# Turned outputs of a retention head ahead of three products, gated outputs in pairs, angle tables one stage earlier

## The chip, the cores and the metric

One core of one Trainium2 chip runs one layer of a decoder trunk. The metric is the time of one execution on the device in microseconds; of several runs the median counts. Profiles are of one execution.

## The reference, cut to what matters

The layer has two branches on the same normalised input (512 tokens, 1024 channels), then an output projection, an MLP and a gated input embedding. The change touches the retention branch, the start of the stage of the other branch's projection, and the start of the output projection:

```python
rq = rope(rq.reshape(B, S, RET_HEADS, RET_QK_DIM), pos)
rk = rope(rk.reshape(B, S, RET_HEADS, RET_QK_DIM), pos) * (RET_QK_DIM ** -0.5)
ro = retention(rq, rk, rv)          # 4 heads, key width 256, value width 512
ro = rms_norm(ro, ret_norm.reshape(RET_HEADS, RET_V_DIM)).reshape(B, S, RET_V_W)
a_ret = (ro * jax.nn.silu(rg)) @ w_br
...
a_mla = mo @ w_bm                   # mo: output of the 8-head latent attention
mixed = jax.nn.sigmoid(gr) * a_ret + jax.nn.sigmoid(gm) * a_mla
x = x + mixed @ w_o
```

`rope` turns the two halves of each head's query and key by cosines and sines of position times frequency; for the retention heads these are the angle tables of this document.

## The kernel before, in words

Every product is of float32 values split into two parts: ScalarE rounds a tile to its high part (lines 262, 307, 310), VectorE takes the remainder as its low part (266, 268, 308, 313), and TensorE does three matmuls (low by high, high by low, high by high) into one PSUM bank. Weights come as chunks of 512 KB through SyncE's and GpSimd's DMA queues into six raw buffers and are split into three pairs of buffers (`wh_...`, `wl_...`). A full product of one weight chunk is 24 matmuls.

The program is a list of steps in an order written out by hand. Each step names the weight chunk that it uses; when the list is run, the chunk of the next step is asked for ahead of the step. Matmuls, and some transfers and table functions, are held in program order (`keep_in_program_order`). The order of all else on each engine is made by a planner, which takes what is ready, the earlier in the program first. PSUM has eight banks under one tag (`psum`, line 162), most activations share 43 buffers of one tag (`dyn`).

The stages around the change, in order of time:

- Latent attention, head by head; the last gate products `gr`; then the projection `bm` of the attention output in eight steps (`branch_m`), with the input x loaded, scaled and split again between them (`norm_x`, tiles `xr`, `xn`). `ret_angles` loads the positions (`posr`) and reduces the angles (`trig`, tiles `tra`, `trk`), `ret_sincos` takes sine and cosine on ScalarE and makes the table `tab`. They stand after steps 2 and 4 of `bm`.
- Retention, two heads at a time (`for q in range(RH // 2)`). For all heads but the first, query and key come from a seven-product scheme: `qk(h, p)` is one product, p being 1, 7, 2, 6, 5, 4, 3 in some order, of 24 matmuls of 256 columns each; products 2, 5, 4 and 3 finish a block of query or key, which VectorE turns with the angle table (763, 847 to 855) and which is then split (`rqx`, `rqy`, `rkx`, `rky`). `seven("rv", ...)` and `seven("rg", ...)` are the same for values and gates, two weight chunks to each product.
- A head goes through `ret_scores`, `ret_attend` (four output blocks `o` and their sums of squares), `ret_gated` (four instructions on VectorE, line 891: output by norm by gate), `ret_turned` (16 transposes `ot` into four banks, each split into `rog` tiles with the norm's gain, lines 310 and 313) and `branch(h, 0..3)` (`branch_r`, products with `w_br`, added up over the heads in DRAM for all but the last).
- After the last head the parts are mixed (`mix`, tiles `mix0` to `mix7`), and the output projection `wo` begins with half a product of its first two chunks (`out_part`).

In the loop, `ret_turned(h)` of the first head of a pair stands right ahead of its branch, behind qk products 5, 4 and 3 of the next head. `ret_turned` of the second head of the first pair stands one product ahead of its branch, and its gated outputs ahead of all products of the next pair.

Of the kernel before, what the change touches and what calls it, by code (L numbers as in the profile page):

```python
# [40 lines left out]
RH, RQK, RV = 4, 256, 512  # L41
# [107 lines left out]
def trunk_layer(ctx: ExitStack, tc: tile.TileContext, xT, pT, pos, gains, const, decay, wstream, outT):  # L149
# [52 lines left out]
    offset, o = {}, 0  # L202
# [5 lines left out]
    def step(key, fn, *args):  # L208
        steps.append((key, fn, args))
# [675 lines left out]
            d["o"].append(o)  # L885
        d["r"], _ = mean_rsqrt(f"ro{h}", ss.rearrange("p (b c) -> p b c", c=1), RV)

    def ret_gated(h):
        d = R[h]
        for b in range(4):  # L890
            STT(d["o"][b], d["o"][b], d["r"][:, b:b + 1], d["z"][b], op0=ALU.mult, op1=ALU.mult)

    def ret_turned(h):
# [260 lines left out]
    def fill(n=1):  # L1154
        for _ in range(n):
            if fillers and fillers[0][0] is None:
                step(*fillers.pop(0))
            if fillers:
                step(*fillers.pop(0))
# [77 lines left out]
    step(None, attend, MH - 1)  # L1237
    step(None, mo_split, MH - 2)
    fill(len(fillers))
    step(None, norm_x, 0)  # L1240
    step(None, norm_x, 1)
    step(None, mo_split, MH - 1)
    for n in range(8):
        step(("bm", n), branch_m, n)
        if n < 6:
            step(None, norm_x, 2 + n)
        if n in (2, 4):
            step(None, ret_angles if n == 2 else ret_sincos)
        if n == 3:
            step(None, x_operand, 7)  # L1250
    for p in (1, 2, 4):
        step(None, x_operand, p)
    def qk(h, *ps):
        for p in ps:
            step(("sw", ("qk", h), p, 0), ret_qk7, h, p)

    def seven(kind, q, *ps):
        for p in ps:
            for c in range(2):
                step(("sw", (kind, q), p, c), ret_seven, kind, q, p, c)  # L1260

    def branch(h, *ks):
        for k in ks:
            step(("br", h, k), branch_r, h, k)


    for q in range(RH // 2):
        h = 2 * q
        if q:
            qk(h, 1, 7, 2, 6)  # L1270
            step(None, ret_turned, h - 1)
            qk(h, 5)
            branch(h - 1, 0)
            qk(h, 4, 3)
            branch(h - 1, 1)
            seven("rv", q, 1)
            branch(h - 1, 2)
            step(None, ret_scores, h)
            seven("rv", q, 7, 2, 6)
            branch(h - 1, 3)  # L1280
        else:
            for key in ("rq", "rk"):
                for n in range(2):
                    step((key, h, n), ret_qk, h, key, n)
            for p, x in ((1, 6), (7, 5), (2, 3)):
                seven("rv", q, p)
                step(None, x_operand, x)
            seven("rv", q, 6)
            step(None, ret_scores, h)
        seven("rv", q, 5, 4, 3)  # L1290
        seven("rg", q, 1)
        step(None, ret_attend, h)
        seven("rg", q, 7, 2, 6)
        qk(h + 1, 1, 7)
        seven("rg", q, 5)
        qk(h + 1, 2)
        seven("rg", q, 4)
        step(None, ret_gated, h)
        qk(h + 1, 6)
        seven("rg", q, 3)  # L1300
        qk(h + 1, 5, 4, 3)
        step(None, ret_turned, h)
        branch(h, 0, 1)
        step(None, ret_scores, h + 1)
        step(None, odd_v, h + 1)
        branch(h, 2, 3)
        step(None, ret_attend, h + 1)
        step(None, ret_gated, h + 1)
    for n in range(8):
        step(None, reload, n)  # L1310
    for n in range(EARLY, 8):
# [2 lines left out]
            step(None, ret_turned, RH - 1)  # L1314
    for k in range(4):
        step(("br", RH - 1, k), branch_r, RH - 1, k)
        step(None, mix, 2 * k)
        step(None, mix, 2 * k + 1)
    for n in range(2):
        step(("o", n), out_part, n, 0)  # L1320
    for n in range(8):
        step(("o", n), out_proj, n)
    step(None, open_tail)
# [106 lines left out]
```

## Time and profile before

| | |
|---|---|
| median of 3 runs | 1125.55 us (1125.17 to 1126.24) |
| profiled execution, its own time | 1122.77 us |
| its span, first to last instruction | 1121.0 us |
| TensorE busy | 1096.8 us (98%) |
| VectorE busy | 730.2 us (65%) |
| ScalarE busy | 558.1 us (50%) |
| mean granted clock of TensorE | 0.993 of full |

The share of an engine is its busy time over the span. The time of a run is a little longer than the span, since it holds what lies before the first and after the last instruction. The granted clock is what the throttle let through, 1.00 being full speed.

### The profile page before, as it was taken

What the parts mean: (1) busy time and instruction counts of PE and PEld (TensorE: products, weight loads), DVE (VectorE), ACT (ScalarE), POOL (GpSimd) and SP (SyncE); (2) the same over time, 40 slices, a digit from 0 to 9 for tenths busy, and PEclk for the clock granted to TensorE, in tenths of its full rate; (3) what the DMA queues carried; (4) which work ended last, traced back from release to release, by engine and by line L of the source; (5) the groups of instructions that cost most, each with busy time, mean ns of one, the idle gap of its engine ahead of it and who ended that gap; (6) DMA issues with size and microseconds to landing.
All of it is one profiled execution on the core that took longest, in us unless ns stands there. A gap on an engine that the chain in (4) does not pass through costs nothing. (4 is left out here: it accounts for less than half of the span.)

```text
span 1121.0 us, 14372 instructions
## 1 busy us (share of the span) xinstructions
PE 1096.8 (98%) x5353; PEld 920.0 (82%) x5353; DVE 730.2 (65%) x1178; ACT 558.1 (50%) x805; POOL 100.6 (9%) x133
## 2 busy tenths in 40 slices
PE   9999999999999989999998999999999999999998
PEld 7878888887788868888886887888888888888887
DVE  7697587557784763765477368555466566668685
ACT  7637555545455644554554634334443443445552
POOL 0000000001112102122110200010100100101000
PEclk9999999999999989999998999999999999999999
DMA  7242232366778865498894944693855755738511
GB/s 258 67 137 75 79 87 85 123 227 205 184 208 224 225 200 153 140 237 215 204 224 165 243 151 153 204 270 116 173 162 171 173 167 155 184 130 211 146 57 57
DMA packets 62166, 186.18 MB, mean 166 GB/s; under 512 B 7632, under 2 KB 9040, under 8 KB 61840
## 3 DMA queue, kind: packets, MB, share of 16 engines
q1 hardware_dynamic: 45744, 131.49, 34.5%
q0 software_dynamic: 16208, 53.75, 24.7%
q8 instruction: 42, 0.69, 0.2%
q14 instruction: 28, 0.23, 0.1%
q10 hardware_dynamic: 144, 0.03, 0.0%
HBM read 166.10 MB, written 17.04 MB: 163 GB/s over the span
## 5 line engine op out<-in xcount | busy, mean ns | idle before, releaser
L169 PE MATMUL dn<-wh_dn,cl 128*128 128x512 f32 x224 | 87.2, 389 | 0.0
L169 PE MATMUL dn<-wh_dn,ch 128*128 128x512 f32 x224 | 87.1, 389 | 0.0
L169 PE MATMUL dn<-wl_dn,ch 128*128 128x512 f32 x224 | 87.1, 389 | 0.0
L262 ACT ACTIVATE wh_dn<-wr_dn 128x1024 fp32r<-128x1024 f32 x32 | 34.0, 1062 | 75.4 <-PE up L169 54.3
L262 ACT ACTIVATE wh_up<-wr_up 128x1024 fp32r<-128x1024 f32 x32 | 34.0, 1061 | 57.7 <-PE up L169 29.3
L266 DVE TENSOR_TENSOR wl_dn<-wr_dn,wh_dn 128x1024 fp32r<-128x1024 f32 x32 | 39.0, 1220 | 27.5 <-ACT wh_dn L262 27.5
L266 DVE TENSOR_TENSOR wl_up<-wr_up,wh_up 128x1024 fp32r<-128x1024 f32 x32 | 39.1, 1222 | 18.6 <-ACT wh_up L262 18.6
L169 PEld LDWEIGHTS dn<-wh_dn,ch 128*128 128x128 f32 x224 | 42.0, 188 | 8.8
L1022 DVE SCALAR_TENSOR_TENSOR f<-up,bcx 128x512 f32<-128x512 f32 x32 | 20.6, 686 | 44.0 <-PE up L169 44.0
L169 PEld LDWEIGHTS dn<-wl_dn,ch 128*128 128x128 f32 x224 | 42.0, 188 | 8.7
L169 PEld LDWEIGHTS dn<-wh_dn,cl 128*128 128x128 f32 x224 | 42.0, 188 | 8.6
L224 POOL DMA_DIRECT2D dr_dn<-wstream x24 | 21.5, 894 | 289.6 <-DMA dr_dn<-wstream 165.7
L262 ACT ACTIVATE wh_dn<-dr_dn 128x1024 fp32r<-128x1024 f32 x24 | 25.5, 1061 | 42.1 <-PE up L169 29.0
L266 DVE TENSOR_TENSOR wl_dn<-dr_dn,wh_dn 128x1024 fp32r<-128x1024 f32 x24 | 29.4, 1223 | 22.4 <-ACT wh_dn L262 22.4
L262 ACT ACTIVATE wh_rv<-wr_rv 128x1024 fp32r<-128x1024 f32 x28 | 29.6, 1058 | 25.7 <-PE rv L169 10.6
L262 ACT ACTIVATE wh_rg<-wr_rg 128x1024 fp32r<-128x1024 f32 x28 | 29.6, 1058 | 25.6 <-PE rg L169 18.9
L266 DVE TENSOR_TENSOR wl_rg<-wr_rg,wh_rg 128x1024 fp32r<-128x1024 f32 x20 | 24.5, 1226 | 23.3 <-ACT wh_rg L262 23.3
L266 DVE TENSOR_TENSOR wl_rv<-wr_rv,wh_rv 128x1024 fp32r<-128x1024 f32 x20 | 24.4, 1223 | 16.0 <-ACT wh_rv L262 16.0
L1080 DVE TENSOR_TENSOR d<-d,dn 128x1024 f32<-128x1024 f32 x24 | 29.3, 1219 | 6.4 <-PE dn L169 6.4
L266 DVE TENSOR_TENSOR wl_br<-wr_br,wh_br 128x1024 fp32r<-128x1024 f32 x16 | 19.5, 1221 | 20.2 <-ACT wh_br L262 20.2
L262 ACT ACTIVATE wh_qk<-wr_qk 128x1024 fp32r<-128x1024 f32 x21 | 22.3, 1063 | 19.7 <-DMA wr_qk<-wstream 7.3
L911 ACT ACTIVATE rt<-br 128x512 f32<-128x512 f32 x24 | 14.0, 595 | 33.1 <-PE br L169 30.7
(1928 smaller groups left out, 3569.5 us busy)
## 6 DMA issues: line engine op xcount, KB each, us to landing
wr_up<-wstream SPq DMA_DIRECT2D x32, 512.0 KB, 4.3
wr_dn<-wstream SPq DMA_DIRECT2D x32, 512.0 KB, 3.5
dr_dn<-wstream POOLq DMA_DIRECT2D x24, 512.0 KB, 7.8
wr_rv<-wstream SPq DMA_DIRECT2D x20, 512.0 KB, 4.6
wr_rg<-wstream SPq DMA_DIRECT2D x20, 512.0 KB, 4.8
wr_rv<-wstream POOLq DMA_DIRECT2D x16, 512.0 KB, 7.6
wr_rg<-wstream POOLq DMA_DIRECT2D x16, 512.0 KB, 7.5
wr_br<-wstream SPq DMA_DIRECT2D x16, 512.0 KB, 5.1
```

What stands on the lines that cost most here:

```text
L169: return tc.keep_in_program_order(nc.tensor.matmul(*a, **k))
L224: nc.gpsimd.dma_start(raw, chunk(("w", blk, kb, fb, c)), accum_op=ALU.add)
L262: i = ACT(hi, raw, AF.Copy, scale=sign)
L266: TT(lo, raw, hi.bitcast(F32), op=ALU.subtract)
L911: ACT(t, ps, AF.Copy)
L1022: STT(u[:, i], ps[:, i], 0.0, V["bcx2"], op0=ALU.max, op1=ALU.mult)
L1080: TT(to, to, dps[p], op=ALU.add if sign > 0 else ALU.subtract)
```

## The change

Four things move; no instruction's shape changes. The angles of the retention tables are reduced ahead of the `bm` stage, and the sines and cosines are taken after its first step. At the start of the second pair the gated outputs of head 1 are made two at a time between the products, their transposes stand behind product 2, and a value product and product 6 lie between them and the branch; branch chunks 1 and 2 follow product 3. In each pair the first head's transposes move ahead of products 5, 4 and 3. In the output projection the first half product stands ahead of the last two mixes in the list.

```diff
-    def ret_gated(h):
+    def ret_gated(h, bs=(0, 1, 2, 3)):
         d = R[h]
-        for b in range(4):
+        for b in bs:
             STT(d["o"][b], d["o"][b], d["r"][:, b:b + 1], d["z"][b], op0=ALU.mult, op1=ALU.mult)
...
     fill(len(fillers))
+    step(None, ret_angles)
     step(None, norm_x, 0)
     step(None, norm_x, 1)
     step(None, mo_split, MH - 1)
...
         step(("bm", n), branch_m, n)
         if n < 6:
             step(None, norm_x, 2 + n)
-        if n in (2, 4):
-            step(None, ret_angles if n == 2 else ret_sincos)
+        if n == 0:
+            step(None, ret_sincos)
...
         if q:
-            qk(h, 1, 7, 2, 6)
+            qk(h, 1)
+            step(None, ret_gated, h - 1, (0, 1))
+            qk(h, 7)
+            step(None, ret_gated, h - 1, (2, 3))
+            qk(h, 2)
             step(None, ret_turned, h - 1)
-            qk(h, 5)
+            seven("rv", q, 1)
+            qk(h, 6)
             branch(h - 1, 0)
-            qk(h, 4, 3)
-            branch(h - 1, 1)
-            seven("rv", q, 1)
-            branch(h - 1, 2)
+            qk(h, 5, 4, 3)
+            branch(h - 1, 1, 2)
             step(None, ret_scores, h)
             seven("rv", q, 7, 2, 6)
             branch(h - 1, 3)
...
         seven("rg", q, 3)
+        step(None, ret_turned, h)
         qk(h + 1, 5, 4, 3)
-        step(None, ret_turned, h)
         branch(h, 0, 1)
         step(None, ret_scores, h + 1)
         step(None, odd_v, h + 1)
         branch(h, 2, 3)
         step(None, ret_attend, h + 1)
-        step(None, ret_gated, h + 1)
+    step(None, ret_gated, RH - 1)
...
     for k in range(4):
         step(("br", RH - 1, k), branch_r, RH - 1, k)
+        if k == 3:
+            step(("o", 0), out_part, 0, 0)
         step(None, mix, 2 * k)
         step(None, mix, 2 * k + 1)
-    for n in range(2):
-        step(("o", n), out_part, n, 0)
+    step(("o", 1), out_part, 1, 0)
```

## Rows read from the trace of the kernel before

**Rows 1.** The page's busy table, TensorE: busy us, share, instructions.
```profile
PE 1096.8 (98%) x5353; PEld 920.0 (82%) x5353; DVE 730.2 (65%) x1178; ACT 558.1 (50%) x805; POOL 100.6 (9%) x133
```
**Rows 2.** Waits of TensorE, whole span: us in total, times, longest.
```profile
PE br L169 <- ACT rog02h L310: 3.2, 1, 3.2
...
PE rq L169 <- ACT xn7h L307: 2.5, 1, 2.5
...
PE br L169 <- DVE rog11l L313: 0.8, 1, 0.8
```
**Rows 3.** Windows: stretch, busy us (instructions) by engine, PEclk, DMA share, GB/s.
```profile
414.00:420.00 6.00, 5.21 (x12) 3.74 (x13) 2.11 (x4) 1.05 (x2) 1.44 (x2) 0.50 0.74 166
420.00:426.00 6.00, 6.00 (x28) 4.97 (x27) 1.23 (x1) 2.14 (x3) 1.11 (x2) 1.00 0.33 115
280.00:285.00 5.00, 3.90 (x16) 3.02 (x17) 4.52 (x7) 3.38 (x6) 0.56 (x1) 1.00 0.85 217
397.38:416.12 18.74, 13.67 (x95) 11.62 (x94) 18.00 (x30) 9.68 (x14) 1.73 (x2) 0.92 0.59 168
...
240.00:245.00 5.00, 5.00 (x24) 4.13 (x22) 3.34 (x5) 1.75 (x3) 1.08 (x2) 1.00 0.69 256
```
**Rows 4.** Timeline of TensorE, head 0's turned outputs and branch: start, us, what.
```profile
405.56 1.91 PE L169 MATMUL ot<-cst,o 128*128 128x128 f32 x16
...
420.22 0.40 PE L169 MATMUL br<-rog02h,wl_br 128*128 128x512 f32 x1
...
425.90 0.39 PE L169 MATMUL br<-rog02l,wh_br 128*128 128x512 f32 x1
```
**Rows 5.** Timeline of TensorE, head 2's turned outputs and branch.
```profile
602.04 1.91 PE L169 MATMUL ot<-cst,o 128*128 128x128 f32 x16
...
614.67 0.40 PE L169 MATMUL br<-rog20h,wh_br 128*128 128x512 f32 x1
```
**Rows 6.** Timeline of TensorE, start of the second pair.
```profile
457.10 0.28 PE L169 MATMUL qk<-xn7h,wh_qk 128*128 128x256 f32 x1
458.77 0.39 PE L169 MATMUL qk<-s60h,wl_qk 128*128 128x256 f32 x1 [1.39 <-DVE wl_qk L266]
...
461.74 1.91 PE L169 MATMUL ot<-cst,o 128*128 128x128 f32 x16
463.41 0.36 PE L169 MATMUL qk<-s50h,wl_qk 128*128 128x256 f32 x1
```
**Rows 7.** Timeline of ScalarE, angle tables and head 0's branch.
```profile
275.18 1.28 ACT L492 ACT_TABLE_LOAD   x1
...
412.15 0.63 ACT L307 ACTIVATE rkx1h<-rku 128x512 fp32r<-128x512 f32 x1 [2.72 <-DVE rku L854]
```
**Rows 8.** Timeline of VectorE, angle table and head 1's gated outputs.
```profile
278.32 0.43 DVE L495 TENSOR_SCALAR tab<-tab 128x512 f32<-128x512 f32 x1 [1.48 <-ACT tab L494]
...
454.85 2.74 DVE L891 SCALAR_TENSOR_TENSOR o<-o,ro,z 128x512 f32<-128x512 f32 x4
```
**Rows 9.** Timeline of TensorE, first retention query product.
```profile
277.86 0.39 PE L169 MATMUL rq<-xn6h,wh_rq 128*128 128x512 f32 x1
...
281.94 0.40 PE L169 MATMUL rq<-xn7h,wh_rq 128*128 128x512 f32 x1
```
**Rows 10.** Timeline of SyncE, VectorE and TensorE, start of the projection stage.
```profile
228.06 0.42 SPq L718 DMA_DIRECT2D xr<-xT  x1
...
231.28 0.69 DVE L308 TENSOR_TENSOR mos7l<-mo,mos7h 128x512 fp32r<-128x512 f32 x1 [0.90 <-ACT mos7h L307]
...
234.80 0.39 PE L169 MATMUL bm<-mos7l,wh_bm 128*128 128x512 f32 x1
```
**Rows 11.** Window of the instructions on the angle tile alone: VectorE, ScalarE.
```profile
250.00:270.00 20.00, 4.09 (x7) 0.00 (x0) 1.00 0.55 195
```
**Rows 12.** DMA issues, 215 to 290: KB each, median us to landing.
```profile
posr<-pos SPq DMA_DIRECT2D x1, 256.0 KB, 3.8
```
**Rows 13.** Timeline of TensorE, start of the output projection.
```profile
687.23 0.50 PE L169 MATMUL wo<-mix0h,wl_o 128*128 128x512 f32 x1 [0.56 <-DVE wl_o L266]
```

## The prediction

> **What bounds the kernel now.** I read the page's busy table first: TensorE is busy 98% of the span [rows 1]. That says where to look, not what is to be had: a matmul at half clock counts as busy too. So the second view is TensorE's waits, where the longest lines touch code that the diff moves [rows 2]: the branch of heads 0 and 2 waits 3.2 us for the split of the third turned block (two such lines, rog02h and rog22h; one stands there), the first retention query product waits 2.5 us for xn7h, and the branch of head 1 0.8 us for rog11l. Third come the windows [rows 3]: the granted clock is 0.50 (1.2 GHz) over 414 to 420, with 12 matmuls where the next 6 us, at 1.00 (2.4 GHz), hold 28. It fell after TensorE had stood for the 3.2 us, and it is 1.00 in 280 to 285 although a wait of 2.5 us ended there. So a wait here costs itself, and the longest two cost the slow matmuls behind them as well. The timeline then gives each loss whole: the start of a matmul against where the pace would have put it. The pace is 25 matmuls from 420.22 to 425.90, 0.227 us each [rows 4].
>
> **The loss at head 0.** The turned outputs start at 405.56. Their 16 transposes take 1.67 us where nothing disturbs them (461.74 to 463.41, [rows 6]), so the branch could start at 407.2, and its 19th matmul at 407.2 + 18 x 0.227 = 411.3. It starts at 420.22 [rows 4]. Loss 8.9 us.
> **At head 2** the same: 602.04 + 1.67 + 14 x 0.227 = 606.9 for the 15th matmul, which starts at 614.67 [rows 5]. Loss 7.8 us.
>
> The reason is the order on the two engines that split. ScalarE stood 2.72 us ahead of 412.15 for VectorE's rotary sum rku [rows 7], and rog02h was queued behind the splits of it. VectorE is nearly full there: 18.0 us of work in 18.74 us [rows 3].
>
> **What the change does there.** Matmuls are held in program order, so the transposes surely move ahead of products 5, 4 and 3. The three take 3 x 2.9 us: one product runs from 458.77 to 461.74 [rows 6]. At head 0 the transposes then start at 405.6 - 8.6 = 396.9, end at 398.6, and the branch may start at 407.2, as in the undisturbed count above. That leaves 8.6 us for four splits. VectorE's work is unchanged, only ordered anew: 18.0 us from 397.4 on ends at 415.4. Retention scores, the next to need its results, start two branch chunks after 407.2, at 407.2 + 48 x 0.227 = 418.1. It fits by 2.7 us. Ahead of the branch itself about half of the 18 us has to be done (four splits, two rotary blocks, three weight remainders: some 10 us, my estimate from that row) in 9.8 us. So a little may be left: between nothing and 3.2 us, the longest wait of this kind. I take 0.5, since need and room agree to some tenths. Gains: 8.4 and 7.3 us.
>
> **The second pair (head 1).** The first matmul after the third product could start 0.12 us after 457.10; it starts at 458.77 [rows 6]. That is 1.55 us, and with rog11l's 0.8 [rows 2] the loss is 2.3 us. wl_qk was late because VectorE did all four gated outputs first, 2.74 us from 454.85 [rows 8]. Splitting them into pairs does not shorten them: they still end at 457.6 at best, and now the transposes stand right behind the third product, at 457.2, and need all four. So 0.4 us of wait stays; at worst the old 1.55 us comes back, through a weight remainder between the pairs, or through banks (three open product banks, four turned ones, and two that the value product then opens make nine, of eight). I take 0.8, nearer the low end, as the value product's weights are asked for two chunks ahead and the first bank clears with VectorE's next work. The wait for rog11l goes: the value product (24 x 0.227 = 5.4 us) and product 6 (2.9 us) now lie between. Gain 1.5 us.
>
> Here a rule speaks against the change. The rows show the window behind the 2.5 us wait at a clock of 1.00 [rows 3], and the product behind the 1.4 us wait at full pace, 24 matmuls in 2.97 us [rows 6]. The Trainium skill (TensorE: Matmul & The Clock Gate, "A second HAM failure mode: psum-queue depth-cycling") says that frequent short idling between groups, while PSUM banks are cycled, makes the clock swing between its levels. By the rows the short waits that I leave cost only themselves; by the rule each place could cost the half clock's share again (a rival below).
>
> **Angle tables.** The third matmul of the stalled group could start at 277.86 + 3 x 0.227 = 278.5; it starts at 281.94 [rows 9]. Loss 3.4 us. In front of xn7h lay, on ScalarE, a table load of 1.28 us [rows 7], two sines and a square, and another load; on VectorE the table's last step stood 1.48 us for them, to 278.32 [rows 8], with the scaling of x's last chunk behind it. All that moves to the first step of the other branch's stage, and the angles ahead of the stage, with their SyncE transfer of the positions (ahead of the first x chunk) and seven VectorE instructions of 4.1 us on the angle tile [rows 11], besides the cast, one rounding step and the last step of the table. Without the 1.48 us alone, xn7h would be ready at about 278.1, when it is wanted. I leave 0.2 us of 0 to 0.6. At the new place ScalarE is busy 1.75 of 5 us and VectorE 3.34 [rows 3]; weights there are split well ahead, so the tables are covered. If that cover were gone they would cost about what they cost now. The number of table loads stays. Gain 3.2 us.
>
> **Output projection.** The order on TensorE stays; asking for the second chunk of weights ahead of the last two mixes takes away a wait of 0.56 us [rows 13], between nothing and all. I take 0.5. The two mixes behind are wanted 2 us later.
>
> **Sum.** 8.4 + 7.3 + 1.5 + 3.2 + 0.5 = 20.9 us. From the profiled execution's 1122.77 us (span 1121.0) that gives 1101.9; it ran 2.8 us below the median of the runs, so against the median I forecast 1125.55 - 20.9 = 1104.7 us. With every loss gone except the 0.4 us: 8.9 + 7.8 + 1.9 + 3.4 + 0.6 = 22.6, or 1102.9.
>
> **The rivals.**
> 1. *The wait comes back at the retention scores.* VectorE is full, so what no longer delays the branch could delay the rotary splits that the scores need. For: 2.7 us of room only. Against: the work is no more, and weights are queued evenly. It decides when VectorE falls more than 2.7 us behind; if it then also halves the clock, one head's gain is lost: 1104.7 + 8 = 1113.
> 2. *The splits don't move.* VectorE's and ScalarE's orders are the planner's. If it puts the splits behind the rotary work as now, TensorE waits at the branch as now: 1104.7 + 15.7 = 1120.4. Against: in program order they now stand three products earlier, and their input is ready 8.6 us earlier. This is the way in which the change would not do what it says.
> 3. *The angles delay mos7.* If VectorE takes the whole chain ahead of the split of mos7 (now at 231.28; TensorE wants it at 234.80, [rows 10]), with positions issued when x's first chunk is now, at 228.06, and landing 3.8 us later [rows 12]: 228.1 + 3.8 + 4.1 + 0.7 = 236.7, a new wait of 1.9 us or a little more: 1107.
> 4. *The clock swings on the short waits.* At head 0, 8.9 us were lost to waits of some 5 and a slow stretch of some 4; once or twice that: 1108.5 to 1112.5. The rule above is this one; against it stands the window at 1.00 after 2.5 us.
> 5. *Slower than before.* VectorE's queue is in order. Should the planner put the first angle step into head 7's softmax, VectorE would stand until the positions land, at about 232, since their transfer is queued on SyncE behind weight transfers until 228 [rows 10]. TensorE would stand with it, and then run some 4 us at half clock. It decides where this outweighs the gain: when VectorE stops before 232 + 4 - 20.9 = 215. At 210 it would give 1130. Against: the chunk of x that takes the same kind of buffer is used on VectorE only after mos7.
>
> **How the numbers follow.** Forecast 0.66; rival 1 0.10, 2 0.06, 3 0.08, 4 0.04, 5 0.03; for small losses elsewhere that add up to no change 0.03. The forecast's own range is 1102 to 1107.5 (the bounds of the left-over waits). The range reaches over rivals 3 and 4 and one head of rival 1, to 1113; down to 1101.3, all losses gone and a run 1.6 us short, within the 2.8 us by which the profiled one was. Rival 2 and 5 are left out. Faster by over 0.2% (2.3 us, about what can be told from no change): 0.94; within it 0.03; slower 0.03.
>
> **What would show it.** Right: no wait for a rog tile over 1 us; granted clock 1.00 in all windows from 390 to 620; no wait for xn7h; a wait of 0.4 to 1.5 us at the transposes of head 1; wl_o gone; TensorE busy time down by the slow matmuls, idle time by the rest. Wrong: waits for rkx, rky or wl_br after the moved transposes (rival 1); rog waits as now (2); a wait for mos7 (3); a clock below 1 with waits under 2 us (4); a wait in head 7's transposes (5).

## The result and the profile after

The changed kernel takes 1113.36 us, the median of four runs (1111.45 to 1115.12), against 1125.36 us for the kernel before in the same runs: a ratio of 0.9898 (0.9873 to 0.9922). It is faster, but by 12.0 us instead of the 20.9 forecast, and 0.4 us above the upper end of the range. Its profiled execution took 1115.12 us (span 1113.3), so against the profiled execution of before 7.65 us are to be found in the traces.

TensorE's waits, in us in total, times, longest (first the whole span, then 430 to 520):

```profile
PE rq L169 <- ACT xn7h L307: 5.6, 1, 5.6
PE rq L169 <- ACT xn6h L307: 2.2, 1, 2.2
...
PE qk L169 <- DVE wl_qk L266: 0.8, 1, 0.8
PE ot L169 <- DVE o L891: 0.7, 2, 0.3
PE rv L169 <- DVE qk L763: 0.5, 1, 0.5
```

The rog waits of [rows 2] and the wl_o wait of [rows 13] are gone. The wait for xn7h, which the change was to remove, has grown from 2.5 to 5.6 us, and xn6h waits as well. The windows, with the columns of [rows 3]:

```profile
280.00:285.00 5.00, 1.15 (x3) 0.40 (x3) 1.27 (x2) 0.63 (x1) 0.57 (x1) 0.77 0.89 207
285.00:290.00 5.00, 3.05 (x7) 2.12 (x8) 4.21 (x8) 2.16 (x4) 0.00 (x0) 0.50 0.42 163
290.00:295.00 5.00, 5.00 (x17) 3.98 (x16) 2.55 (x4) 1.08 (x3) 1.08 (x2) 0.71 0.47 168
400.00:420.00 20.00, 20.00 (x133) 18.26 (x132) 15.87 (x25) 11.18 (x15) 0.86 (x1) 1.00 0.71 223
460.00:480.00 20.00, 18.71 (x111) 16.06 (x109) 12.75 (x18) 9.50 (x13) 3.50 (x5) 1.00 0.58 154
600.00:620.00 20.00, 20.00 (x116) 17.78 (x115) 17.41 (x31) 9.35 (x14) 3.46 (x4) 1.00 0.58 157
```

Around heads 0 and 2 (400 to 420, 600 to 620) TensorE is busy without a gap at 1.00. The slow stretch now lies at 282 to 293, in the first retention query product. TensorE's timeline there, and at the second pair:

```profile
273.29 0.39 PE L169 MATMUL bm<-mos7h,wh_bm 128*128 128x512 f32 x1
...
279.92 0.50 PE L169 MATMUL rq<-xn6h,wl_rq 128*128 128x512 f32 x1 [2.16 <-ACT xn6h L307]
...
286.95 0.79 PE L169 MATMUL rq<-xn7h,wl_rq 128*128 128x512 f32 x1 [5.58 <-ACT xn7h L307]
...
296.17 0.39 PE L169 MATMUL rk<-xn0h,wl_rk 128*128 128x512 f32 x1
...
467.63 0.39 PE L169 MATMUL qk<-s60h,wl_qk 128*128 128x256 f32 x1 [0.76 <-DVE wl_qk L266]
```

Reading the same landmarks of TensorE in both traces gives the time place by place. The loss of the first query products, called the stage's loss below, is the first key matmul's start, less the last bm matmul's start and 49 matmuls of 0.227 us: before, 287.62 - 273.10 - 11.11 = 3.41 us; after, 296.17 - 273.29 - 11.11 = 11.77. The two landmarks in the trace of before:

```profile
273.10 0.39 PE L169 MATMUL bm<-mos7h,wh_bm 128*128 128x512 f32 x1
...
287.62 0.39 PE L169 MATMUL rk<-xn0h,wl_rk 128*128 128x512 f32 x1
```

| place | before, us | after, us | gain | forecast |
|---|---|---|---|---|
| up to the end of bm | 273.10 | 273.29 | -0.2 | 0 |
| first query products, loss | 3.41 | 11.77 | -8.4 | 3.2 |
| first key product to head 1's scores (head 0's branch) | 139.41 | 130.59 | 8.8 | 8.4 |
| head 1's scores to head 2's (second pair) | 67.96 | 69.05 | -1.1 | 1.5 |
| head 2's scores to head 3's (head 2's branch) | 127.39 | 119.81 | 7.6 | 7.3 |
| head 3's scores to the output projection | 61.41 | 61.41 | 0.0 | 0 |
| output projection | 44.39 | 43.52 | 0.9 | 0.5 |

They add up to 7.6 us. The terms for heads 0 and 2 and for the output projection came out 0.3 to 0.4 us above the forecast; two rows have the wrong sign, and the angle tables are 11.6 of the 13.3 us between forecast and ledger.

What is late there is x. The queue of SyncE, first of before, then of after (each line an issue):

```profile
228.06 0.42 SPq L718 DMA_DIRECT2D xr<-xT  x1
...
230.78 0.42 SPq L718 DMA_DIRECT2D xr<-xT  x1
...
231.83 0.38 SPq L718 DMA_DIRECT2D xr<-xT  x1
238.08 0.33 SPq L244 DMA_DIRECT2D wr_rq<-wstream  x1
...
271.52 0.54 SPq L718 DMA_DIRECT2D xr<-xT  x1
```

```profile
228.25 0.42 SPq L508 DMA_DIRECT2D posr<-pos  x1
...
230.97 0.49 SPq L718 DMA_DIRECT2D xr<-xT  x1
238.64 0.33 SPq L244 DMA_DIRECT2D wr_rq<-wstream  x1
239.06 0.38 SPq L718 DMA_DIRECT2D xr<-xT  x1
...
276.21 0.33 SPq L234 DMA_DIRECT2D wr_rv<-wstream  x1
...
277.44 0.33 SPq L718 DMA_DIRECT2D xr<-xT  x1
```

Before, three chunks of x were out when the second wr_rq was issued; after, one. A weight transfer waits until VectorE has taken the remainder out of a raw buffer, one for each step of bm (5.4 us), and every chunk behind it waits with it. The weights wait in both kernels (222 to 285: 23.9 us in six such waits before, 18.2 in five after); what changed is how many chunks stand behind them. The last chunk is issued 5.9 us later, at 277.44, when TensorE needs its split at 278, and it takes 8.0 us to land (5.9 before): VectorE scales it at 285.49.

```profile
SPq L244 <- DVE wl_bm L266: 18.2, 5, 5.0
```

```profile
277.85 0.69 DVE L706 TENSOR_TENSOR gb<-gb,bm 128x512 f32<-128x512 f32 x1 [1.67 <-ACT gb L705]
...
285.49 0.75 DVE L719 SCALAR_TENSOR_TENSOR xr<-xr,gn,rbc 128x512 f32<-128x512 f32 x1 [2.99 <-DMA xr<-xT]
```

The first of these is SyncE's own waits, the second VectorE's timeline. The tables themselves were done by 255.3 us; their cover on VectorE and ScalarE held. What had none was the order of the transfers.

### The profile page after: what moved, and what is told of

Read it like the earlier page. It is cut to its first block, busy times and chain, and to the rows that moved or that the text cites. A ratio compares the mean times of both kernels' runs of the same rounds, so it can differ in the third digit from the quotient of the medians.

```text
span 1113.3 us, 14378 instructions
## 1 busy us (share of the span) xinstructions
PE 1094.0 (98%) x5353; PEld 918.8 (83%) x5353; DVE 730.3 (66%) x1178; ACT 558.1 (50%) x805; POOL 100.3 (9%) x133
## 4 chain that ended last, share of the span: by engine, by line
PE 90%; DVE 4%; DMA 3%; ACT 2%; issue 1%; SPq 0%; POOL 0%; DVEq 0%; ACTq 0%
PE up L169 16%; PE dn L169 14%; PE br L169 7%; PE rg L169 7%; PE rv L169 7%; PE qk L169 5%; PE pg L169 4%; PE gr L169 4%; PE wo L169 4%; PE gm L169 4%; PE bm L169 2%; PE sc L169 2%; PE ro L169 2%; PE pcq L169 1%; PE rs L169 1%; PE mo L169 1%
## 5 line engine op out<-in xcount | busy, mean ns | idle before, releaser
L262 ACT ACTIVATE wh_rv<-wr_rv 128x1024 fp32r<-128x1024 f32 x28 | 29.8, 1067 | 29.8 <-PE rv L169 11.6
L262 ACT ACTIVATE wh_rg<-wr_rg 128x1024 fp32r<-128x1024 f32 x28 | 29.6, 1058 | 27.1 <-PE rg L169 17.7
L657 ACT ACTIVATE p<-p,ng,hr 128x128 f32<-128x128 f32 (+3 forms) x32 | 20.6, 645 | 10.4 <-DVE ng L655 10.3
L262 ACT ACTIVATE wh_br<-wr_br 128x1024 fp32r<-128x1024 f32 x16 | 17.0, 1060 | 17.4 <-PE qk L169 8.4
```

What stands on the lines that cost most here:

```text
L262: i = ACT(hi, raw, AF.Copy, scale=sign)
L657: ACT(cols[b], cols[b], AF.Exp, bias=ng[:, b:b + 1], scale=d["rq"][:, b], accum_out=sums[:, b:b + 1])
```

## The experiments

The theory formed from these traces: the four tiles of the angles (`posr`, `posrf`, `tra`, `trk`) take four of the 43 shared activation buffers at the moment when x's first chunks need them, so the planner puts these chunks behind weight transfers. The planner's own reasons are not on record; the runs show the order that it made and what that costs. Rivals: the place that the positions' transfer takes at the head of the queue; the table work on VectorE and ScalarE; the reordered steps after the stage. Times are medians; a ratio is to the kernel before on the same chip.

**Tables back** in their old place, all else of the change kept:

```diff
-    step(None, ret_angles)
...
-        if n == 0:
-            step(None, ret_sincos)
+        if n in (2, 4):
+            step(None, ret_angles if n == 2 else ret_sincos)
```

> The changed kernel with the angle tables where they stood before (after steps 2 and 4 of the projection); everything else of the change stays. Theory: the moved tables alone cost the missing time, since their four tiles take activation buffers that x's chunks had, so that these are issued behind more weight transfers on SyncE's queue. Then this kernel is faster than the changed one: 1125.4 less 8.4, 7.3, 1.5 and 0.5 us is 1107.7, less up to 1.5 us; no wait for xn6h or xn7h over 2.5 us. Rival: the reordered steps after the stage cost it, or gain less than forecast; then it stays at 1113.

1107.69 us (1106.9 to 1108.0), ratio 0.9848 (0.9836 to 0.9861): what the theory gave. The other parts are worth 17 us by themselves (17.7 were forecast). Against this kernel the moved tables cost the changed one 5.7 us. With the 3.2 us that they were to gain this makes 8.9 us, which is by how much the median missed (20.9 less 12.0).

**Tables moved alone**, the reverse edit in the kernel before.

> The kernel before with the tables' move alone. Theory (buffers): slower than before by what the changed kernel lost at the first retention query product, some 8 to 9 us, so about 1134, with waits for xn6h and xn7h of about 2 and 5.6 us and a clock below 1 in 280 to 295. Rival (the tables are not to blame): 1122 to 1126.

1130.65 us (1130.01 to 1131.45), ratio 1.0054 (1.0042 to 1.0066), with waits of 5.8 us for xn7h and 1.9 for xn6h and a stage's loss of 11.68 us. The move alone makes the kernel slower, by 6.1 us rather than 8 to 9; the last section gives a part of the reason.

**Turned outputs alone**, the first heads' transposes moved in the kernel before.

```diff
+        step(None, ret_turned, h)
         qk(h + 1, 5, 4, 3)
-        step(None, ret_turned, h)
```

> The kernel before with one part of the change alone: the first head's transposes ahead of products 5, 4 and 3, in both pairs. Forecast by the terms for heads 0 and 2: 1124.6 less 8.4 and 7.3 us is 1108.9, no wait for a rog tile over 1 us, clock 1.00 from 390 to 640. Rival (part of the gain belongs to the gated outputs in pairs and to the second pair's order): 1112 or more.

1107.91 us (1107.81 to 1108.15), ratio 0.9849 (0.9835 to 0.9862); no rog tile of heads 0 and 2 is waited for, and 400 to 420 and 600 to 620 run at 1.00. That is 1.0 us below the forecast. This one edit gives as much as everything but the tables together.

**The positions' transfer on GpSimd's queue**, buffers as in the changed kernel.

```diff
-        nc.sync.dma_start(again, pos.partition_broadcast(P))
+        nc.gpsimd.dma_start(again, pos.partition_broadcast(P))
```

> The changed kernel with the positions' transfer on GpSimd's queue instead of SyncE's; the four angle tiles hold their buffers as in the changed kernel. Theory (buffers): x's chunks keep their places behind the weight transfers, the wait for xn7h stays at about 5 us, 1112 to 1114. Rival (the slot: it is the positions' own place at the head of SyncE's queue that pushed x's chunks down): about 1105.

1114.15 us (1112.39 to 1115.13), ratio 0.9905 (0.9892 to 0.9918), stage's loss 10.99 us. The waits are 4.7 us for xn6h and 2.6 for xn7h, where about 5 for xn7h were expected, but they add up to nearly as much as after. Taking the positions off the queue doesn't help: their slot is not the cause.

**Angles in the table's own tile**, no activation buffer taken.

```diff
     def trig(name, posf, inv):
-        ang, kf = T(name + "a"), T(name + "k")
         if name == "tr":
-            V["tab"] = dyn.tile([P, 2, S], F32, tag="tab", name="tab", bufs=1)
             c_, s_ = V["tab"][:, 0], V["tab"][:, 1]
+            ang, kf = c_, s_
         else:
+            ang, kf = T(name + "a"), T(name + "k")
...
     def ret_angles():
-        again, posf = dyn.tile([P, S], I32, tag="t", name="posr"), T("posrf")
+        V["tab"] = dyn.tile([P, 2, S], F32, tag="tab", name="tab", bufs=1)
+        again, posf = V["tab"][:, 0].bitcast(I32), V["tab"][:, 1]
```

> The changed kernel with the angles reduced in the table's own tile: the positions land in its first half, the rounding steps work in both halves, and no activation buffer is taken. Same instructions. Theory (buffers): x's chunks are issued as early as in the kernel before, no wait for xn6h or xn7h is left, and the whole gain of 3.2 us comes on top of the others: 1102 to 1105. Rival (the tables' work on VectorE and ScalarE ahead of the stage is what delays): 1110 to 1114.

1113.13 us (1111.85 to 1115.68), ratio 0.9901 (0.9889 to 0.9913). By the time alone the theory falls, but the trace shows another wait: a tile that nothing else uses is free from the start, and the planner put the positions and the first angle steps there. VectorE stood for them in its queue until 17.0 us, early in the kernel. The remainder wl_a behind them ran at 17.97, though the rounding that it needs had ended at 11.5. Here VectorE works strictly in order, as the Trainium skill says of it (TensorE: Matmul & The Clock Gate, "Architectural detail: the array is 16× 32×32, not 1× 128×128"). TensorE stood behind it; the first line is VectorE's waits, the second TensorE's:

```profile
DVE tab L510 <- DMA tab<-pos: 5.7, 1, 5.7
```

```profile
PE pA L169 <- DVE wl_a L266: 6.0, 1, 6.0
```

bm ends at 281.03, 7.7 us later than after. The stage's loss fell from 11.77 to 4.35 us and the wait for xn6h was gone; 1.9 us of wait for xn7h stayed, which the theory had not expected. So this run can't be read by its total; the next one takes one buffer, which is not free that early.

**One buffer**: the positions land in an activation buffer, all later steps work in the table's tile. Place and slot are those of the changed kernel.

```diff
-        again, posf = V["tab"][:, 0].bitcast(I32), V["tab"][:, 1]
+        again, posf = dyn.tile([P, S], I32, tag="t", name="posr"), V["tab"][:, 1]
```

> The changed kernel with one activation buffer instead of four taken by the angles: the positions land in a buffer, all later steps work in the table's own tile. The positions are still issued ahead of x's first chunk. Theory (buffers that push x's chunks behind weights): x's chunks 2 to 7 are issued one weight transfer earlier than in the changed kernel, the waits for xn6h and xn7h are gone or under 1 us, 1101 to 1105. Rival (the early table work or the positions' place on SyncE's queue delays): 1109 to 1114.

1107.33 us (1106.66 to 1107.85), ratio 0.9843 (0.9829 to 0.9856): 6 us from three buffers, which falls between the theory's range and the rival's. The chunks of x from the second on are issued one weight transfer earlier than after, as expected, but TensorE still waits 2.4 us for xn7h. Its chunk was issued at 271.44, as early as before, and took 7.3 us to land (5.9 before), until 278.7. VectorE then came to it 0.5 us later, behind a gate's product:

```profile
278.63 0.69 DVE L707 TENSOR_TENSOR gb<-gb,bm 128x512 f32<-128x512 f32 x1 [2.71 <-ACT gb L706]
279.24 0.75 DVE L720 SCALAR_TENSOR_TENSOR xr<-xr,gn,rbc 128x512 f32<-128x512 f32 x1
```

The gate of that product had been issued at 270.97 and took 7.0 us to land. So two late transfers hold the scaling: the chunk's own until 278.7, and the gate's, whose product VectorE has to finish first, until 279.2. A store of a gate went out beside both at 271.37; whether that made them slow was not tested.

**One buffer, another place**: angles after step 1 and sines after step 3.

```diff
-        if n == 0:
-            step(None, ret_sincos)
+        if n in (1, 3):
+            step(None, ret_angles if n == 1 else ret_sincos)
```

> As the kernel with one buffer, but with the angles after step 1 and the sines after step 3 of the projection, between the old place and the new. Theory: x's chunks are issued as early as in the kernel before, and the sines are out of the way of x's last chunk: 1101 to 1105, the rest of the wait of 2.5 us gone. Rival (xn7h is late by its transfer alone, the tables' place is not in its way): the wait stays at 2 us or more, 1106 to 1109.

1104.08 us (1102.98 to 1105.76), ratio 0.9815 (0.9800 to 0.9830). Stage's loss 0.93 us; the window that was at 0.77 is whole:

```profile
280.00:285.00 5.00, 5.00 (x24) 4.12 (x23) 2.42 (x3) 1.06 (x1) 0.00 (x0) 1.00 1.02 327
```

This beats both kernels. VectorE scales x's last chunk at 277.18, 1.48 us earlier than before, which is what the prediction's term for the tables counted on. The theory gave the right time, but its reason is only half of it: against the kernel with one buffer the sines were out of the way already, and what differs is that both transfers land sooner, the gate after 4.3 us instead of 7.0 and the chunk, issued at 271.62, after 5.1 instead of 7.3 (the gate's store goes out at 276.16 here). That the new place made the transfers faster is not shown.

**The same place with four buffers** (the one-buffer edit undone).

> The kernel with angles after step 1 and sines after step 3 that took 1104.1 us, but with the four activation buffers of the changed kernel instead of one. Theory (the buffers push x's chunks behind weight transfers): x's chunks from the fifth on are issued one weight transfer later, and 2 to 8 us come back, 1106 to 1112, with waits for xn6h or xn7h. Rival (only the place of the tables counts): 1103 to 1105.

1111.46 us (1110.23 to 1113.92), ratio 0.9875 (0.9855 to 0.9895). At one place, with the same work, three buffers more cost 7 us. TensorE's waits, and the issue of x's last chunk, 271.62 in the kernel with one buffer:

```profile
PE rq L169 <- ACT xn7h L307: 5.8, 1, 5.8
```

```profile
277.10 0.33 SPq L718 DMA_DIRECT2D xr<-xT  x1
```

This pair and the pair of the changed kernel and its one-buffer form carry the theory: at either place the table work is the same, and the number of buffers alone moves the chunks on the queue and the time.

**x's chunks on GpSimd's queue**, in the changed kernel.

```diff
         t = T(f"xr{k}")
-        nc.sync.dma_start(t, xT[:, k])
+        nc.gpsimd.dma_start(t, xT[:, k])
```

> The changed kernel with x's eight chunks issued on GpSimd's queue instead of SyncE's; the angle tiles and their buffers as in the changed kernel. Theory (x's chunks are late because they are issued in order behind weight transfers that wait for a raw buffer): on a queue without weight transfers in this stage they come in time, the waits for xn6h and xn7h go, 1102 to 1107. Rival (the buffers themselves are not free earlier, or the DMA engines are too crowded): the waits stay, 1110 to 1115.

1114.89 us (1114.36 to 1115.29), ratio 0.9910 (0.9897 to 0.9922), stage's loss 12.91 us. What was expected of the queue fails. Four chunks went out together from 229.29 on, but the last one again late, behind a gate's store that waits for VectorE (GpSimd's timeline):

```profile
279.11 0.56 POOL L355 DMA_DIRECT2D am4d<-gb  x1 [0.72 <-DVE gb L706]
279.65 0.55 POOL L718 DMA_DIRECT2D xr<-xT  x1
```

So another busy queue is no cure. That four chunks could go out by 231.6, with the four angle tiles filled by 233.3, says that the early chunks did not lack buffers while this kernel ran; how the number of buffers enters the order that the planner makes was not read. Whether the later chunks waited here for a buffer or only for the store ahead stays open, and a queue with nothing else on it wasn't tried.

**The second pair** as it was before, in the best kernel so far.

> The kernel that took 1104.1 us, with the second pair's order as it was before: gated outputs in one go, transposes of head 1 behind product 6, the value product behind product 3. Forecast of the prediction's step for this pair: its gain of 1.5 us is lost, 1105.6. New theory, from the traces: VectorE has no gap there from the first gated output to the weight remainder, so the order only moves the wait, and the new one costs about 0.5 us more in all: 1103.6, with a wait for wl_qk of about 1.6 and for rog11l of 0.8 us.

1103.56 us (1102.24 to 1104.73), ratio 0.9808 (0.9790 to 0.9826): the forecast wanted it slower, and it is within the spread of the kernel that it came from. Its wait for wl_qk is 2.2 us, and none for rog11l is left (1.6 and 0.8 were expected). By the traces the stretch from head 1's scores to head 2's takes 69.16 us here and 68.52 in the kernel with the new order, so here the new order did not cost 0.5 us, it gained 0.6; between the kernels with the turned outputs alone (old order) and with the tables back (new order) it lost 0.5 (68.21, 68.76). With the kernel that it came from it is the fastest one run.

**The second pair and the output projection alone**, in the kernel before.

> The kernel before with the second pair's order and the output projection's half product alone. Forecast of the prediction's two steps: 2.0 us faster, a ratio of 0.998. New theory: the second pair gives 0.5 us away and the output projection 0.9 us, so 0.4 us faster, a ratio of 0.9996, which can't be told from none.

1124.05 us (1121.09 to 1125.48), ratio 0.9989 (0.9979 to 0.9999). Both figures lie in the interval; the times don't tell them apart. By the trace the second pair's stretch took 67.82 us, against 67.96 before: neither 1.5 us gained nor 0.5 us lost. The output projection took 43.52 us, as in the changed kernel.

**Two gated outputs of head 1 left out.**

> The kernel that took 1104.1 us, without the gated outputs of blocks 2 and 3 of head 1 (these two instructions are left out, so those blocks go ungated into the branch). VectorE's order there stays otherwise. Theory (VectorE without a gap sets the start of the second pair's branch): 1.33 us less of its work takes away the waits at the transposes (0.7 us) and shortens the waits for qk (0.5) and wl_qk (0.8): head 2's scores start 1 to 1.4 us sooner after the first query and key product than in that kernel. Rival (the banks or the transfers set it): the waits for qk and wl_qk stay, and only the 0.7 us goes.

From the first query and key product to head 2's scores it took 45.43 us (439.58 to 485.01), against 46.74 (438.33 to 485.07) in the kernel with all four: 1.31 us less, for 1.33 us of VectorE's work. The waits are not those that the theory gave: the two at the transposes are gone, that for qk fell from 0.5 to 0.3, that for wl_qk stayed at 0.8. VectorE's chain, first and last link:

```profile
444.47 0.17 DVE L420 TENSOR_SCALAR ro1a<-ss 128x4 f32<-128x4 f32 x1 [5.51 <-ACT sqo L885]
...
455.75 1.21 DVE L266 TENSOR_TENSOR wl_qk<-wr_qk,wh_qk 128x1024 fp32r<-128x1024 f32 x1
```

Product 6 starts at 457.02, as soon as this remainder is there. The stretch follows VectorE; which name a wait has only says where TensorE ran into it. The other profiles agree. From the first step of VectorE's chain to head 2's scores it is 41.85 to 42.07 us in all nine of them with the new order and all four gated outputs, though the chain starts between 4.13 and 4.90 us after the pair's first product; here it is 40.54. The execution as a whole took 1104.22 us, no less than with all four, since it lost 1.5 us ahead of the pair.

**The kernel before once more.**

> The kernel before once more, for one look. Theory: after the same wait of 2.5 us for xn7h the clock falls to 0.50 in some executions and stays at 1.00 in others, so this profile may show 0.66 in 280 to 285 (and about 2 us more time, 1124 to 1126) where the first one showed 1.00 (1122.8). Rival: the clock behind this wait belongs to the kernel, and is 1.00 again.

1123.68 us. The same wait of 2.55 us, but the clock in the window behind it is 0.66, not the 1.00 of [rows 3]:

```profile
280.00:285.00 5.00, 3.92 (x10) 2.80 (x11) 3.90 (x7) 3.12 (x5) 0.56 (x1) 0.66 0.94 218
```

The stage's loss is 4.56 us instead of 3.41. The whole came out 0.9 us longer, less than expected.

## Why the prediction failed, step by step

**The step that failed is the term for the angle tables.** It counted the tables' work on ScalarE and VectorE, named as cover that "weights there are split well ahead", and allowed 0 to 0.6 us. That cover held. Moved along with the instructions were a transfer and four buffers, and neither had a price in the term. The prediction did see the transfer "ahead of the first x chunk", but followed it only to mos7l (rival 3), which was split at 231.47, ahead of the angles, without delay. It did not follow the seven other chunks of x, which share the buffers and the queue: 3.2 us of gain became 8.4 us of loss by the traces, and 5.7 to 6.1 us by the medians. With three of the four buffers given back and a place two to three steps later, the term is obtained: 1104.1 us, 3.6 us less than with the tables in their old place. That this lies so near the 1104.7 that was forecast is in part luck, since the second pair gave nothing and the other terms a little more than forecast.

**Half of that step was wrong in another way too.** "Without the 1.48 us alone, xn7h would be ready at about 278.1": in the one-buffer kernel the table is out of the way and xn7h still starts at 280.0, held by two late transfers; its chunk alone landed only at 278.7. The prediction left the chunk's own landing out. Before, it landed at 277.4, later than the 277.2 at which the scaling could start without the 1.48 us, and scaling (0.74) and rounding (0.61) come behind it, so 278.8 was the best. The table's last step was the last of two waits, not the only one.

**Heads 0 and 2 were right**, in mechanism and size: 8.8 and 7.6 us for 8.4 and 7.3. The 0.5 us left for the splits of the turned blocks was hardly needed; rivals 1 and 2 did not come.

**The second pair gave nothing, where 1.5 us was forecast.** By the ledger the stretch lost 1.1 us, in three parts. The pair's first product starts 0.5 us later after head 1's scores (22.10 us, 21.56 before). VectorE's chain of work, from the norm's first step on, starts 1.0 us later after that product (4.88 us, 3.87 before). From the chain's start to head 2's scores it is 0.5 us less (42.07 us, 42.53 before). The last part is the order's own, and it has the sign that the prediction gave it: the five profiles with the old order show 42.53 to 42.98 us, the nine with the new one 41.85 to 42.07. It is smaller than forecast because VectorE has no gap from the norm's first step to wl_qk (453.74 to 467.57). So the waits that went (1.4 and 0.8 us) came back at the transposes, the value product and product 6, 2.0 us by the view of waits, and in more pieces: the prediction put the end of the gated outputs at 457.6 at best and left 0.4 us at the transposes, but these took 2.82 us (457.50 to 460.32) with two waits of 0.34, where 1.67 was counted. The two losses come from ahead of this: the gated outputs began 7.27 us after the pair's first product (448.86, 456.13), 1.0 us later than before (448.59, [rows 8]), since ScalarE had waited for head 1's last values, reloaded on GpSimd's queue behind one more weight transfer:

```profile
435.45 0.91 POOL L224 DMA_DIRECT2D wr_qk<-wstream  x1 [6.51 <-DVE rv10l L308]
...
439.48 0.90 POOL L810 DMA_DIRECT2D rv13l<-v3d  x1
```

The values took 7.3 us to land, against 5.7 before. That this transfer is the reason was read from the trace alone, and whether the pair's new order makes the chain start late stays open: it starts 3.76 to 4.62 us after the first product with the old order and 4.13 to 4.90 with the new one.

**The output projection** gave 0.9 us, above the bound of 0.56 us: the 192 matmuls now take 43.52 us, which is 0.227 us each and no loss, so the 0.3 us of restart behind the wait went with it.

**Rival 4** (the clock swings on short waits, after the Trainium skill's TensorE: Matmul & The Clock Gate, "A second HAM failure mode: psum-queue depth-cycling") did not decide: with waits of 0.3 to 0.8 us the windows 440 to 460 and 460 to 480 stay at 1.00, so these waits brought no such swing. But the row that was set against it, 1.00 behind 2.5 us, was one execution's.

**Rival 5** did not come here, but the run with the angles in the table's tile shows its mechanism: VectorE standing on the positions for 5.7 us, early in the kernel.

## What to carry to other kernels

A step that is moved takes its buffers and its place in each queue along. Before pricing a move, list what shares its buffer tag and its DMA queue in the new place, and follow the last of these to its consumer: here it was not the moved work that came late, but the eighth chunk of an input, 50 us further on. Where an engine has no gap, a new order mostly renames the wait (here it made 0.5 to 1 us); less work or an earlier start of its chain makes time.

## What the runs showed that was not expected

One wait, the same code and the same length, costs two different amounts. Behind the wait of 2.55 us for xn7h the granted clock stayed at 1.00 in the first profile of the kernel before; in the second one, and in the kernels with the tables back, with the turned outputs alone and with the second pair alone, it fell to 0.50 for some 3 us, and their windows 280 to 285 show 0.66. By the stage's loss this costs 1.2 to 1.6 us (4.56 to 4.98 in these four, against 3.41). Behind waits of 2.4 us (one buffer) and 1.9 us (angles in the table's own tile) it fell to 0.50 as well; behind one of 0.9 us (the second pair as before) it stayed at 1.00. The profiled execution of before was one that had been spared, and that of after is the slowest of its four runs. That is likely part of why 1122.77 lay 2.8 us below the median, and why moves measured by medians and by profiles differ here (12.0 and 7.65 us for the change; 6.1 by medians and 8.3 by the stage's loss for the tables' move alone, or 6.7 to 7.1 against the four that were not spared). What decides whether the clock falls, no run shows.
